# A decoder layer's start: products of x that the norm has not scaled yet, for the first two of eight groups

## The chip, the cores and the metric

The kernel runs on one core of one Trainium2 chip. Its time is device microseconds (us) of one execution. The kernel before the change was run three times: 2462.48, 2463.01 and 2464.7 us, a median of 2463.01. A further execution was taken with the hardware profiler; every row below is from that one.

The engines are named as the profile names them: PE is TensorE (matrix products; PEld its weight loads), DVE is VectorE, ACT is ScalarE, POOL is GpSimd, SP is SyncE, whose queue issues the DMAs.

## What is computed

One layer of a decoder on 1024 prompt tokens and 8 x 8 sample tokens, 1088 in all, with a model width of 2048. The input is normalised and modulated by a scale and a shift that depend on the batch element, then multiplied by one wide input projection; attention, a gated MLP and an mLSTM follow, and an output projection. Only the beginning matters here:

```python
def _rmsnorm(x, g):
    xf = x.astype(jnp.float32)
    y = xf * lax.rsqrt(jnp.mean(xf * xf, axis=-1, keepdims=True) + EPS)
    return (y * g.astype(jnp.float32)).astype(x.dtype)

def _layer(x, c, norm_g, ada_w, ada_b, w_in, ...):
    mod = jax.nn.silu(c.astype(f32)) @ ada_w.astype(f32) + ada_b.astype(f32)
    shift, scale, gate = jnp.split(mod, 3, axis=-1)
    h = (_rmsnorm(x, norm_g).astype(f32) * (1.0 + scale[:, None]) + shift[:, None]).astype(dt)
    proj = h @ w_in
    ...
```

So h = x * r * s + b, with r one factor per token (the norm's), s and b one number per model row and batch element (nine of them: the prompt, and eight sample sequences). The product with the weights is a sum over the 2048 model rows. Because r does not depend on the row, it can be taken out of the sum, and so can the share of b: sum(w * (x*r*s + b)) = r * sum(w * x*s) + sum(w * b).

## The kernel before

**Layout.** x lies transposed: 16 tiles `xs[k]` of 128 model rows by 1088 tokens, 544 KB each. Tokens are worked in three chunks (`CH`: 384, 384 and 320 wide; the last holds the 64 sample tokens). PE multiplies in fp32r, a rounded format; for fp32 accuracy every factor is split into a high and a low part (`wh`, `wl` of the weights, `hH`, `hL` of h), and `products` takes three products: high by high, low by high, high by low. The split of a weight tile is an ACT cast (`wh`, L98) and a POOL subtraction (`wl`, L99) of 128x512.

**The first stage.** The first four column tiles of the projection (`NST` = 4, kept in SBUF sums `accs`) are computed while scale and shift are still being made, in eight groups: group g covers the rows of tiles 2g and 2g+1. One group is 12 units (4 column tiles by 3 chunks) of six matmuls, and after each unit DVE adds the result to its sum (L584). Group 0 is taken in two halves, one row tile at a time (L553).

**Scale and shift.** `ada_group(g)` is a generator that the loops advance step by step. It multiplies the 8 tiles of `adaw` for the group (512 KB each) by the silu of c on PE (L342, "sets" of two tiles; the two halves of group 0 are L353), copies the result (ACT L366), turns it (PE L374), reduces it (DVE L376), makes scale and shift (`modulation`, DVE L409 to L411), applies them to the two x tiles (DVE L420 to L424, then ACT cast to `hH`, L425) and makes `hL` (DVE L431). The table `AT[g]` says behind which unit of group g which later group's generator takes a step.

**The norm's factor.** At the program's start all 16 x tiles are loaded, squared (ACT L389 and DVE L387 by turns) and summed over rows by PE (`token_sums`, L272); `token_rsqrt` makes the factor and spreads it over the partitions (`rbc`). `scaled(k)` multiplies an x tile by it: two on DVE, the other 14 on POOL (L398). Only then come the modulation and the first product.

**Order.** Every engine runs its instructions in the order in which the program wrote them. SP issues all DMAs in such an order too; an issue whose tile is still in use waits, and all behind it wait with it. The `ad` tiles have 4 buffers, the raw weights 4, the split weights 4, the PSUM tiles of products (`mm`) 4.

## Time and profile before

| | us |
|---|---|
| median of 3 runs | 2463.01 |
| profiled execution, its own time | 2462.13 |
| its span, first to last instruction | 2460.1 |
| first product of the first stage begins | 47.22 |
| group 2 (the third) begins its products | 100.99 |
| group 3 (the fourth) begins its products | 119.45 |
| bytes moved by DMA | 332.95 MB |
| granted TensorE clock, mean | 0.997 |

A row of the timeline reads: start, duration, engine, line, operation, output <- inputs, shapes, count; in brackets the idle time before it and what ended it. A row of the windows reads: the stretch, its length, then for each engine busy us and in brackets the instructions, the granted PE clock, the busy share of the DMA engines and the rate in GB/s. A row of the groups reads: line, engine, operation, tiles, shapes, count | busy us, mean ns of one | idle before, and for whom. Durations of instructions that follow each other on one engine can overlap a little, so a row of several is shorter than count times mean.

### The profile page before, as it was taken

The page shows a single profiled execution, that of the slowest core. Times are in us where ns is not written, and L with a number is a line of the kernel's source. Part 1 is how long each engine was busy: PE and PEld are TensorE (multiplying, and loading weights), DVE is VectorE, ACT ScalarE, POOL GpSimd, SP SyncE. Part 2 cuts the span into 40 slices and gives each one's busy share as a digit, 9 for nine tenths or more (in the row PEclk, how much of TensorE's full clock was granted, in tenths as well). Part 3 has the DMA queues.
Part 4 walks back from the last instruction along what each step waited for, and adds up shares of the span by engine and source line. Part 5 has one row for each costly group of instructions (what it writes and reads, how often), then busy time and mean ns, then how long its engine had stood idle before and what let it go on. Part 6 is the DMA issues. An engine that isn't in the chain of part 4 may idle for free.

```text
span 2460.1 us, 39820 instructions
## 1 busy us (share of the span) xinstructions
PE 2419.0 (98%) x15879; PEld 2237.5 (91%) x15879; DVE 923.8 (38%) x2489; ACT 746.1 (30%) x1638; POOL 644.3 (26%) x502
## 2 busy tenths in 40 slices
PE   5899999999999999999999999999999999999999
PEld 2677899999999999999999999888989999999898
DVE  5662300323232231323352001333311688887322
ACT  3222221323323232323321111222212566666210
POOL 2431222232322232222221322121211333332321
PEclk8999999999999999999999999999999999999999
DMA  8774621111121112112411524657565855554454
GB/s 289 255 258 158 220 65 44 57 62 57 54 65 58 53 49 73 38 52 71 127 56 59 172 76 171 223 178 265 188 240 187 255 157 165 152 151 139 164 171 141
DMA packets 157081, 332.95 MB, mean 135 GB/s; under 512 B 21770, under 2 KB 76834, under 8 KB 149216
## 3 DMA queue, kind: packets, MB, share of 16 engines
q1 hardware_dynamic: 156896, 330.41, 41.1%
q8 instruction: 125, 2.05, 0.3%
q14 instruction: 60, 0.49, 0.1%
HBM read 284.26 MB, written 54.55 MB: 138 GB/s over the span
## 4 chain that ended last, share of the span: by engine, by line
PE 95%; DMA 2%; DVE 2%; issue 0%; SPq 0%; ACT 0%; POOL 0%; DVEq 0%; POOLq 0%; ACTq 0%
PE mm L252 27%; PE mm L254 26%; PE mm L253 26%; PE pt L1493 2%; PE ad L342 2%; PE os L1300 1%; PE o L1504 1%; PE sq L1250 1%; PE o L1502 1%; DMA ad<-in_adaw 1%; PE s L1452 1%; PE s L1451 1%; DMA x<-in_xT 1%; PE b L942 0%; PE b L974 0%; PE b L982 0%
## 5 line engine op out<-in xcount | busy, mean ns | idle before, releaser
L252 PE MATMUL mm<-hH,wh 128*128 128x384 f32 (+1 forms) x3168 | 1058.5, 334 | 9.3 <-ACT hH L425 8.1
L253 PE MATMUL mm<-hL,wh 128*128 128x384 f32 (+1 forms) x3168 | 1034.8, 327 | 2.6 <-DVE hL L431 2.6
L254 PE MATMUL mm<-hH,wl 128*128 128x384 f32 (+1 forms) x3168 | 1036.0, 327 | 0.0
L99 POOL TENSOR_TENSOR wl<-wraw,wh 128x512 fp32r<-128x512 f32 x344 | 445.7, 1304 | 1545.8 <-ACT wh L98 1433.4
L252 PEld LDWEIGHTS mm<-hH,wh 128*128 128x128 f32 x3168 | 595.9, 188 | 51.3 <-issue 32.1
L253 PEld LDWEIGHTS mm<-hL,wh 128*128 128x128 f32 x3168 | 596.3, 188 | 4.4 <-DVE hL L431 3.6
L254 PEld LDWEIGHTS mm<-hH,wl 128*128 128x128 f32 x3168 | 595.4, 188 | 0.0
L98 ACT CAST wh<-wraw 128x512 fp32r<-128x512 f32 x344 | 200.8, 596 | 409.6 <-PE mm L253 270.9
L252 PE MATMUL mm<-yH,wh 128*128 128x512 f32 (+2 forms) x768 | 261.7, 341 | 0.0
L254 PE MATMUL mm<-yH,wl 128*128 128x512 f32 (+2 forms) x768 | 251.7, 328 | 0.4 <-POOL wl L99 0.4
L253 PE MATMUL mm<-yL,wh 128*128 128x512 f32 (+2 forms) x768 | 251.7, 328 | 0.0
L254 PEld LDWEIGHTS mm<-yH,wl 128*128 128x128 f32 x768 | 144.8, 189 | 11.7 <-POOL wl L99 0.9
L252 PEld LDWEIGHTS mm<-yH,wh 128*128 128x128 f32 x768 | 145.1, 189 | 9.6
L253 PEld LDWEIGHTS mm<-yL,wh 128*128 128x128 f32 x768 | 145.3, 189 | 9.3
L898 DVE SCALAR_TENSOR_TENSOR u<-R,cw,u 128x384 f32<-128x384 f32 (+1 forms) x108 | 62.0, 574 | 213.3 <-ACT u L896 210.8
L1588 DVE SCALAR_TENSOR_TENSOR xo<-mm,gate,xo 128x512 f32<-128x512 f32 (+2 forms) x96 | 54.5, 569 | 117.4 <-PE mm L254 101.8
L1494 ACT CAST pH<-pt 128x512 fp32r<-128x512 f32 (+1 forms) x120 | 65.3, 544 | 63.3 <-PE pt L1493 62.5
L1495 DVE TENSOR_TENSOR pL<-pt,pH 128x512 fp32r<-128x512 f32 (+1 forms) x120 | 74.8, 623 | 11.6 <-ACT pH L1494 11.2
L1463 ACT ACTIVATE P<-P,mx 128x128 f32<-128x128 f32 (+3 forms) x96 | 74.4, 777 | 1.0 <-DVE mx L1460 1.0
L1493 PE MATMUL pt<-cst,P 128*128 128x128 f32 x432 | 66.6, 272 | 0.0
L1454 DVE CUSTOM_DVE_ANT_0 P<-s,btab 128x384 f32<-128x384 f32 (+2 forms) x96 | 54.7, 570 | 30.0 <-PE s L1452 29.1
L1504 PE MATMUL o<-pL,vh 128*64 128x256 f32 x240 | 61.8, 281 | 1.9 <-DVE pL L1495 1.9
(324 smaller groups left out, 2378.8 us busy)
## 6 DMA issues: line engine op xcount, KB each, us to landing
wraw<-in_win SPq DMA_DIRECT2D x264, 256.0 KB
ad<-in_adaw SPq DMA_DIRECT2D x96, 512.0 KB
kv<-in_ck SPq DMA_DIRECT2D x30, 1024.0 KB
kv<-in_cv SPq DMA_DIRECT2D x30, 1024.0 KB
wraw<-in_wout SPq DMA_DIRECT2D x48, 256.0 KB
x<-in_xT SPq DMA_DIRECT2D x16, 544.0 KB
yraw<-yD SPq DMA_DIRECT2D x16, 544.0 KB
xo<-in_xT SPq DMA_DIRECT2D x16, 544.0 KB
```

Of the source, the lines that this page charges most:

```text
L98: self.nc.scalar.copy(wh[:, :n], raw[:, :n])
L99: self.nc.gpsimd.tensor_tensor(wl[:, :n], raw[:, :n], wh[:, :n].bitcast(FT), op=OP.subtract)
L252: T.matmul(ps[:, :n], wh[:, a], rh[:, t0:t0 + n], start=first and i == 0, stop=False)
L253: T.matmul(ps[:, :n], wh[:, a], rl[:, t0:t0 + n], start=False, stop=False)
L254: T.matmul(ps[:, :n], wl[:, a], rh[:, t0:t0 + n], start=False, stop=last and i == len(rows) - 1)
L898: V.scalar_tensor_tensor(u[:, :npr], R[:, j:j + npr], cw[:, m, j:j + 1], u[:, :npr], op0=OP.mult, op1=OP.add)
L1454: V.tensor_tensor_reduce(s[:, k0:k0 + w], ps[:, :w], e["bt"][:, x:x + w], 1.0, mx[:, np_ - 1:np_] if np_ else -3.0e38, op0=OP.add, op1=OP.max,
L1463: S.activation(s[:, :nk], s[:, :nk], AF.Exp, bias=mx[:, 2:3], accum_out=mx[:, 3:4])
L1493: T.transpose(pt[:, o:o + 128], P[r][:, k:k + 128], ident)
L1494: S.copy(pH[:, f:], pt[:, f:])
L1495: at(0, 3, lambda: V.tensor_tensor(pL[:, f:], pt[:, f:], pH[:, f:].bitcast(FT), op=OP.subtract))
L1504: T.matmul(po[0][0:64, :256], e["vh"][:, kb, 0, :], pL[:, c], start=False, stop=(kb == 2 * m + 1), skip_group_check=True)
```

## The change

Groups 0 and 1 (`NRAW` = 2) multiply x by the scale alone: `raw_high` and `raw_low` make `rH` and `rL` from x * s. Their products go into the sums unscaled. When the norm's factor is there, DVE multiplies each of the 12 pieces of the sums by it (new line in group 2's loop) and adds the shift's share, `ssum`, which `shift_sums` makes with 16 small matmuls per group. The rows of tiles 0 to 3 are needed as true h later, so `scaled`, `high` and `low` make `hH` and `hL` for them during groups 3 to 7.

Squares and their sums move behind the units of group 1 (table `STAT`). In group 2, `high` with `fused` applies scale and factor in one DVE instruction per chunk. `scaled` runs on POOL for all tiles but 4 and 5, in three pieces by chunk. x tiles are loaded in four portions: tile 0 first, tile 1 behind the first four ada tiles, tiles 2 and 3 behind the first half of group 1's ada tiles, and tiles 4 to 15 ahead of most of group 2's. Up to group 4, half of the ada tiles lie in the general slots, so that eight can be on the way instead of four. Groups 0 to 2 take their units by chunk (all four column tiles of a chunk, then the next); before, only group 0 did.

```diff
+    xload(0, 1)
+    W.dma_to(0)
     ada_dma(4)
     W.dma_to(1)
-    for k in range(KT):
...
+    xload(1, 2)
+    ada_dma(8)
...
+    def raw_high(k, c):
...
+        V.tensor_scalar(x[:, a], x[:, a], md[k][:, 1, 0:1], None, op0=OP.mult)
+        if c == 2:
+            per_batch(x, k, 1, OP.mult)
+        S.copy(rH[k][:, t0:t0 + n], x[:, t0:t0 + n])
+
+    def raw_low(k, c):
...
+        V.tensor_tensor(rL[k][:, a], xs[k][:, a], rH[k][:, a].bitcast(FT), op=OP.subtract)
...
+    def scaled(k):
+        for t0, n in CH:
+            a = slice(t0, t0 + n)
+            G.tensor_tensor(xs[k][:, a], xs[k][:, a], rbc[:, a], op=OP.mult)
...
+    def high(k, t0=0, t1=TOK, fused=False):
...
+        if fused:
+            V.scalar_tensor_tensor(x[:, a], x[:, a], md[k][:, 1, 0:1], rbc[:, a], op0=OP.mult, op1=OP.mult)
+        S.activation(hH[k][:, a], x[:, a], AF.Identity, bias=shift(k)[:, 0:1])
...
+    def low(k, t0=0, t1=TOK):
...
+        V.scalar_tensor_tensor(hL[k][:, a], xs[k][:, a], shift(k)[:, 0:1], hH[k][:, a].bitcast(FT), op0=OP.add,
+                               op1=OP.subtract)
...
+    AT[2] = {1: (0, 1), 3: (1,), 4: (0,), 5: (1,), 7: (1,), 8: (1,), 9: (1,), 10: (1,), 11: (1, 2)}
+    AT[3] = {0: (1,), 2: (1,), 4: (1,), 6: (1,), 7: (1,), 8: (1,), 9: (1, 2), 11: (2,)}
...
+    STAT = {(1, 2 * i): (2 * i + 4, 2 * i + 5) for i in range(6)}
+    SCALED = {(2, 0): 6, (2, 2): 7, (2, 6): 8, (2, 9): 9, (3, 1): 10, (3, 4): 11, (3, 7): 0, (3, 10): 1,
+              (4, 1): 12, (4, 4): 13, (4, 7): 2, (4, 10): 3, (5, 1): 14, (5, 4): 15}
...
+            if g == NRAW:
+                V.tensor_tensor(acc, acc, rbc[:, t0:t0 + n], op=OP.mult)
             ps = mm.tile([128, 512], FT, tag="mm", name="mm")
+            products(ps, n, wh[:, a], wl[:, a], hh, t0, True, True)
+            if g != NRAW:
+                V.tensor_tensor(acc, acc, ps[:, :n], op=OP.add)
+            else:
+                m = min(n, NPR - t0)
+                V.scalar_tensor_tensor(acc[:, :m], ps[:, :m], ssum[:, j, 0:1], acc[:, :m], op0=OP.add, op1=OP.add)
...
+            for k, sq in waiting:
+                sums(k, sq)
+            waiting = [(k, square(k)) for k in STAT.get((g, u), ())]
...
+        if g == 1:
+            for k, sq in waiting:
+                sums(k, sq)
+            waiting = []
+            next(root)
+            shift_sums(1, w)
+            next(groups[2])
...
+            G.tensor_copy(shifts[:, 2 * NRAW, 0:1], hL[5][:, 0:1].bitcast(FT))
```

Three places show what moves.

SP's queue at the very start, before the change (`cst` are constants, `csp` the raw c, `x` the x tiles, `ad` the ada tiles, `wraw` raw weights):

```order
L204 DMA cst<-in_cst 128x693
L304 DMA csp<-in_cT 128x16x9
L312 DMA x<-in_xT 128x1088 x16
L326 DMA ad<-in_adaw 128x4x256 x4
L87 DMA wraw<-in_win 128x2x256 x2
L326 DMA ad<-in_adaw 128x4x256 x4
```

The same place in the changed program (`craw` is the raw c, now one contiguous row per partition):

```order
L211 DMA cst<-in_cst 128x693
L311 DMA craw<-in_cT 128x144
L324 DMA x<-in_xT 128x1088
L87 DMA wraw<-in_win 128x2x256
L339 DMA ad<-in_adaw 128x4x256 x4
L87 DMA wraw<-in_win 128x2x256
L324 DMA x<-in_xT 128x1088
L339 DMA ad<-in_adaw 128x4x256 x4
L342 DMA ad<-in_adaw 128x1024 x4
L324 DMA x<-in_xT 128x1088 x2
```

Fifteen of the 16 x tiles have moved behind the first four ada tiles; twelve of them come ten issues after the last row shown.

DVE in the middle of group 2, before (`acc` are the sums, `mm` the products in PSUM; the step of the next group's modulation stands between the adds):

```order
L584 TENSOR_TENSOR acc_232<-acc_232,mm 128x384 x2
L376 TENSOR_REDUCE ads<-at 128x36
L409 TENSOR_TENSOR md<-ads,cst 128x2x9
L410 TENSOR_TENSOR md<-ads,cst 128x2x9
L411 SCALAR_TENSOR_TENSOR md<-md,cst 128x2x9
L420 TENSOR_SCALAR x<-x,md 128x1024
```

DVE in the first half of group 2, now (`rbc` is the norm's factor, `ssum` the shift's share):

```order
L513 SCALAR_TENSOR_TENSOR hL<-x,md,hH 128x384 x2
L702 TENSOR_TENSOR acc_131<-acc_131,rbc 128x384
L709 SCALAR_TENSOR_TENSOR acc_131<-mm,ssum,acc_131 128x384
L702 TENSOR_TENSOR acc_132<-acc_132,rbc 128x384
L709 SCALAR_TENSOR_TENSOR acc_132<-mm,ssum,acc_132 128x384
L499 SCALAR_TENSOR_TENSOR x<-x,md,rbc 128x384 x2
```

One DVE instruction per unit has become two, and the chunks of the group's own h are made between them.

POOL from the first weights on, before (`wl` the low weights, `hL` low parts that POOL made for some chunks):

```order
L99 TENSOR_TENSOR wl<-wraw,wh 128x512 x2
L398 TENSOR_TENSOR x<-x,rbc 128x1088 x4
L431 TENSOR_TENSOR hL<-x,hH 128x384 x2
L431 TENSOR_TENSOR hL<-x,hH 128x320
L99 TENSOR_TENSOR wl<-wraw,wh 128x512 x2
```

And now (the copy into `shifts` only makes POOL wait for the first chunk of group 2's `hL`):

```order
L108 TENSOR_TENSOR wl<-wraw,wh 128x512 x6
L751 COPY shifts<-hL 128x1
L424 TENSOR_TENSOR x<-x,rbc 128x384 x2
L424 TENSOR_TENSOR x<-x,rbc 128x320
L424 TENSOR_TENSOR x<-x,rbc 128x384 x2
```

POOL's scaling of x no longer stands ahead of the first products; it starts inside group 2, in three pieces per tile.

## The prediction

> **What bounds the kernel now.** The page first: busy shares and slices.

> ```profile
> span 2460.1 us, 39820 instructions
> PE 2419.0 (98%) x15879; PEld 2237.5 (91%) x15879; DVE 923.8 (38%) x2489; ACT 746.1 (30%) x1638; POOL 644.3 (26%) x502
> ...
> PE   5899999999999999999999999999999999999999
> ```

> PE is the bound, busy 2419.0 of 2460.1 us. Each digit covers 61.5 us, and only the first two fall below 9: most of the 41 idle us lie early. The windows over the first stage, cut where groups begin, show where.

> ```profile
> core 0: us, PE busy (x) PEld busy (x) DVE busy (x) ACT busy (x) POOL busy (x), PEclk, DMA share, GB/s
> 28.00:47.20 19.20, 9.39 (x83) 4.01 (x83) 12.54 (x19) 4.20 (x9) 9.80 (x5) 0.86 0.95 315
> 47.20:62.50 15.30, 13.76 (x70) 7.85 (x71) 9.44 (x16) 6.76 (x17) 7.42 (x5) 0.73 0.53 161
> 62.50:76.40 13.90, 10.36 (x50) 8.00 (x49) 8.04 (x18) 4.19 (x10) 3.78 (x4) 0.88 0.73 260
> 76.40:101.00 24.60, 21.33 (x127) 13.55 (x126) 14.75 (x31) 5.34 (x9) 13.19 (x10) 1.00 0.59 198
> 101.00:119.40 18.40, 17.75 (x110) 13.05 (x109) 12.93 (x25) 3.90 (x6) 9.15 (x5) 1.00 0.82 296
> 119.40:136.00 16.60, 16.60 (x110) 13.28 (x109) 12.06 (x25) 3.90 (x6) 8.60 (x5) 1.00 0.79 287
> 136.00:152.90 16.90, 16.90 (x110) 13.19 (x109) 11.96 (x25) 3.89 (x6) 8.48 (x5) 1.00 0.78 280
> ```

> From 119.4 on a group takes 16.6 to 16.9 us and PE never rests. Ahead of that, group 0's halves took 15.3 and 13.9 us at granted clocks of 0.73 and 0.88, group 1 24.6, group 2 18.4. What can be won lies ahead of 119.4; from there a lead or a lag goes one to one into the end. So I ask: when does group 3's first unit finish, and what do the groups behind it lose?

> ```profile
> 119.45 0.34 PE L252 MATMUL mm<-hH,wh 128*128 128x384 f32 x1
> ...
> 120.34 0.33 PE L254 MATMUL mm<-hH,wl 128*128 128x384 f32 x1
> ```

> Group 3's first unit is these two and four between, 0.175 apart: before, it was done at 120.6.

> **The change up to group 2.** The old start, in four rows:

> ```profile
> 7.79 1.11 ACT L389 ACTIVATE sq<-x 128x1088 f32<-128x1088 f32 x1 [1.12 <-DMA x<-in_xT]
> ...
> 27.94 0.84 PE L272 MATMUL st<-sq,cst 128*32 128x384 f32 x6 [0.33 <-ACT sq L389]
> ...
> 28.17 1.29 DVE L387 TENSOR_TENSOR sq<-x 128x1088 f32<-128x1088 f32 x1 [1.45 <-DMA x<-in_xT]
> ...
> 47.22 0.69 PE L252 MATMUL mm<-hH,wh 128*128 128x384 f32 x1 [5.45 <-ACT hH L425]
> ```

> Sixteen x tiles of 544 KB landed 1.36 us apart ((28.17 - 7.79)/15), 410 GB/s. Now only x tile 0, 256 KB of weights and four ada tiles (1.3 to 1.4 us each) come ahead of the first scale, so it has its data at 13. Then the chain to a product:

> ```profile
> 39.67 0.64 PE L353 MATMUL ad<-ad,csp 128*32 128x256 f32 x8 [0.63 <-DMA ad<-in_adaw]
> ...
> L366 ACT COPY at<-ad 128x256 f32<-128x256 f32 x16 | 5.3, 376 | 52.3 <-PE ad L342 51.8 <-PE ad L353 0.4
> ...
> 40.24 0.44 PE L374 MATMUL at<-cst,at 128*128 128x128 f32 x2
> ...
> 40.72 0.23 DVE L376 TENSOR_REDUCE ads<-at 128x18 f32<-128x72 f32 x1 [0.31 <-PE at L374]
> ...
> 46.66 0.51 ACT L425 CAST hH<-x 128x384 fp32r<-128x384 f32 x1 [8.01 <-DVE x L420]
> ```

> Set 0.64, copy 0.38, turn 0.44, reduce 0.23, three small DVE instructions about 0.6, scale 0.4, cast 0.51, hand-offs about 0.4: 3.6 us. First product at 16.6, not 47.22.

> Then by steps, as estimates from these rows. First half: 36 products at 0.175 (twice that while the clock is low, 0.73 in the old window) and four sets: 10 us, 26.6. Chain 3.2, second half 9.5, since its adds stand on DVE behind 5 us of `raw_high` and `raw_low`: 39.3. Shift sums 1.6 (16 tiny products, 0.1 each), two sums of squares 1.4, two sets 1.9, chain 3.4: 47.6. Group 1: a pair of units 2.1, two sums of squares 0.65 each; but DVE squares (1.29) behind the add of the pair's first unit, so PE waits some 0.85: 4.25 a pair, six pairs, less 2 for the narrow chunk: 23.5, to 71.1. Last, the root:

> ```profile
> 32.41 0.17 DVE L221 TENSOR_SCALAR rs<-ss 128x9 int32<-128x9 int32 x1
> ...
> 34.25 0.17 DVE L225 SCALAR_TENSOR_TENSOR rs<-rs,rs 128x9 f32<-128x9 f32 x1
> ...
> 34.48 1.86 PE L295 MATMUL rb<-cst,rs 128*128 128x128 f32 x9 [1.75 <-DVE rs L225]
> ```

> Ten steps from 32.41 to 34.42 are 2.0, the spread 1.86; before them copies, shift sums, a set and transposes (3.5), behind them a set, copies, turn and modulation (2.3 with what PE hides): DVE's first fused instruction at 80.8, the first product at 82, **19 ahead** of group 2's old 100.99 (119.45 less the 18.4 of its window). The four chains are known to a second each: 14 to 22.

> The loads hide under this. Ahead of group 2's last ada tile stand 24 MB: at 410 GB/s it lands at about 62, at the 315 of the window with the small pieces at 79, and its set is due at 79. SP's new waits for PE (old ada buffers) stand behind tiles still in flight.

> **Group 2, on DVE.** PE needs some 17 us for it. DVE does not keep up:

> ```profile
> L584 DVE TENSOR_TENSOR acc<-acc,mm 128x384 f32<-128x384 f32 x56 | 30.2, 549 | 23.8 <-PE mm L254 23.6
> ...
> L898 DVE SCALAR_TENSOR_TENSOR u<-R,cw,u 128x384 f32<-128x384 f32 x72 | 44.6, 619 | 203.7 <-ACT u L896 202.0
> ...
> 98.30 1.28 DVE L431 TENSOR_TENSOR hL<-x,hH 128x1088 fp32r<-128x1088 f32 x1
> ...
> 128.30 0.81 DVE L420 TENSOR_SCALAR x<-x,md 128x1024 f32<-128x1024 f32 x1
> ```

> The old add costs 0.549. Now each unit is a rescale at 0.549 and, waiting for it, an add with a scalar like L898's 0.619 (ends overlap by 0.05): 1.13, eight times; the four narrow units, with four instructions, 1.4: 14.6 in all. The group's own h: first chunk 2.4, the other two 5.9. The next group's modulation: 0.9, twice 0.81 + 0.3, twice 1.2, 5.5. Sum **28.4 us** with no wait, in DVE's order, and group 3's first unit needs the last `hL` of it. The old group 2 had 12.93 of DVE.

> To that comes POOL, which scales four tiles and splits two or three weight tiles meanwhile. What that does, the old trace shows:

> ```profile
> 75.12 4.05 POOL L431 TENSOR_TENSOR hL<-x,hH 128x384 fp32r<-128x384 f32 x4
> ...
> 75.30 0.94 DVE L553 TENSOR_TENSOR acc<-acc,mm 128x384 f32<-128x384 f32 x2
> ...
> 76.16 1.20 DVE L420 TENSOR_SCALAR x<-x,md 128x256 f32<-128x256 f32 x1
> ...
> 77.28 1.02 DVE L423 TENSOR_TENSOR x<-x,md 128x64 f32<-128x64 f32 x1
> ...
> 79.50 0.21 DVE L423 TENSOR_TENSOR x<-x,md 128x64 f32<-128x64 f32 x1
> ```

> Four POOL pieces of 384 ran from 75.12 to 79.17. DVE's adds out of PSUM did not notice. L423 took 1.02 under them and 0.21 after: an instruction that lives in SBUF alone waits for one POOL piece. Group 2 has 15 POOL pieces of about 1 us. If DVE's next SBUF instruction always meets one, as here, about 0.65 of each is lost, +9.8; if pieces fall under PSUM adds and gaps, nothing. I take +6, nearer the row: 34.4. Group 3's first unit is done at 80.8 + 34.4 + 0.4 = 115.6, **5 ahead** of 120.6 (1 to 11).

> [...]

> **Behind group 2.** In group 3, POOL has two weight tiles and four x tiles (0, 1, 10, 11), 14 us instead of 8.6. The second pair falls on the chain that makes group 4's h, eleven SBUF instructions, five to seven of which meet a piece; 1.2 us of it are slack: 0 to -4.5, I take -3.5. In groups 4 and 5 the pieces end ahead of the chain, by its unit: 0. The extra `high` and `low` of tiles 0 to 3 lie on ACT and in DVE's free 4.6 us a group. Eight ada tiles on the way instead of four: a group's content is 11.9 of products, 3.85 of sets and 0.44 of turn, 16.2, against 16.6 and 16.9: +1.2 over three groups (0 to 2). PE's clock, idle in group 2:

> ```profile
> 66.27 0.33 PE L253 MATMUL mm<-hL,wh 128*128 128x384 f32 x1
> ...
> 69.10 1.11 PE L374 MATMUL at<-cst,at 128*128 128x128 f32 x4 [2.33 <-ACT at L366]
> ...
> 70.33 0.52 PE L253 MATMUL mm<-hL,wh 128*128 128x384 f32 x1
> ...
> 73.03 0.33 PE L254 MATMUL mm<-hH,wl 128*128 128x384 f32 x1
> ```

> After an idle 2.33 the products took 0.52, and 0.33 again by 73.03. Group 3 may start so: 0 to -1.7, I take -0.7.

> [...]

> **Sum**: 5 - 3.5 + 1.2 - 0.7 = 2 us less than the profiled execution's 2462.13 (its span and 2.03 around it): 2460.1. That execution lay 0.9 below the median of the runs, so **2461**.

> **Rivals.** (a) *The lock costs little*: pieces by chunk fit under PSUM adds, group 2 takes 29 to 30 on DVE, group 3 loses 1. Lead 10 - 1 + 1 - 0.5 = 9.5: about 2453 (2449 to 2457). For it: only 12 of the SBUF instructions of group 2 stand outside the chains, and POOL starts late. Against it: the 1.02 row. (b) *Slower, by the lock*: every SBUF instruction of group 2 meets a piece (38.2), group 3 loses 4.5, the clock 1.7, and the start comes 2 late: lead 1 - 4.5 - 1.7 - 2 + 0.5 = -6.7: about 2469. It ends above the old time once DVE's group 2 lasts over 36 us. (c) *The early start is not there*, for want of data: x behind ada tiles makes group 1 wait. By the 410 GB/s tile 15 lands at 55, needed at 68; only under 315 would it decide: 2466 or so.

> **How the numbers follow.** Forecast 0.41, (a) 0.34, (b) 0.21, (c) 0.04. A measurement can tell 0.2%, 4.9 us: faster is (a), 0.34; slower (b) and (c), 0.25; same 0.41. The range takes in most of (a) and (b): 2450 to 2471; the forecast alone 2458 to 2467.

> **What would show it.** First product near 17 and not 47; group 2's first at 79 to 87; DVE busy without a gap from there for 30 to 38 us while PE falls to about half; rescales of acc longer than 0.55 where POOL runs; group 3's first unit at 110 to 119. I am wrong if group 1 waits for x, or if group 2 goes at PE's pace.

## The result

The changed kernel takes 2484.53 us, median of 4 runs (2482.16 to 2486.69), beside 2463.24 for the kernel before (4 runs): a ratio of 1.0081, 95% interval 1.0069 to 1.0093. It is 21 us slower; the forecast was 2461, with a range up to 2471. The profiled execution ran 2482.16 us, its span 2480.4.

The page of the changed kernel, busy shares and slices of 62 us:

```profile
span 2480.4 us, 39969 instructions
PE 2428.9 (98%) x15911; PEld 2244.8 (91%) x15911; DVE 941.6 (38%) x2550; ACT 752.0 (30%) x1654; POOL 641.7 (26%) x522
PE   7799999999999999999999999999999999999999
```

The first slice rose from 5 to 7, the second fell from 8 to 7. The windows of the changed kernel, cut where group 0's halves, group 1, the chain to the norm's factor and groups 2, 3, 4 and 5 begin:

```profile
core 0: us, PE busy (x) PEld busy (x) DVE busy (x) ACT busy (x) POOL busy (x), PEclk, DMA share, GB/s
18.80:32.40 13.60, 11.78 (x77) 8.14 (x77) 4.78 (x15) 7.15 (x17) 0.00 (x0) 1.00 1.05 394
32.40:50.70 18.30, 15.86 (x100) 11.25 (x100) 11.34 (x29) 4.28 (x10) 2.54 (x2) 0.91 0.84 314
50.70:75.00 24.30, 22.96 (x144) 13.52 (x144) 17.88 (x34) 9.47 (x15) 2.58 (x2) 1.00 0.77 303
75.00:86.70 11.70, 8.43 (x68) 4.42 (x65) 4.65 (x20) 2.92 (x8) 0.00 (x0) 1.00 0.65 222
86.70:114.20 27.50, 21.32 (x116) 14.46 (x116) 24.93 (x49) 5.97 (x13) 16.72 (x15) 0.94 0.78 286
114.20:143.60 29.40, 22.19 (x116) 14.71 (x116) 19.31 (x34) 4.65 (x8) 15.93 (x14) 0.77 0.24 78
143.60:165.10 21.50, 19.33 (x112) 14.31 (x109) 15.21 (x26) 5.76 (x9) 11.94 (x10) 0.92 0.71 238
165.10:183.00 17.90, 17.80 (x110) 12.88 (x108) 13.65 (x26) 5.16 (x8) 14.23 (x14) 1.00 0.79 260
```

The first product is there at 18.8 instead of 47.2, as meant. Then the lead is eaten: group 2 takes 27.5 us (18.4 before), group 3 29.4 (16.6), group 4 21.5 (16.9). In group 3 PE is busy for 22.2 of 29.4 us, and at a granted clock of 0.77. (The 1.00 of the first row is no evidence: the trace's record of the clock begins at 22.3, and PE's products from 18.8 to 22 start 0.32 us apart, as they do at half rate further on.) The starts of products in PE's timeline give the account. The last two rows count only products of 128 by 128 weights:

| first product of | before | changed | lead (-) or lag |
|---|---|---|---|
| group 0 | 47.2 | 18.8 | -28.4 |
| group 1 | 76.4 | 50.7 | -25.7 |
| group 2 | 101.0 | 86.8 | -14.2 |
| group 3 | 119.5 | 114.3 | -5.2 |
| (end of group 3's first unit) | 120.67 | 123.63 | +3.0 |
| group 4 | 136.0 | 143.7 | +7.7 |
| group 5 | 152.9 | 165.1 | +12.2 |
| group 7 | 185.5 | 199.0 | +13.5 |
| 72 products after group 7's first | 214.4 | 229.2 | +14.8 |
| 360 more products on | 299.6 | 319.3 | +19.7 |

Group 3's beginning, in PE's timeline of the changed kernel:

```profile
114.28 0.55 PE L259 MATMUL mm<-hH,wh 128*128 128x384 f32 x1 [4.37 <-ACT hH L525]
118.17 0.69 PE L260 MATMUL mm<-hL,wh 128*128 128x384 f32 x1 [3.35 <-DVE hL L529]
...
122.62 0.69 PE L260 MATMUL mm<-hL,wh 128*128 128x384 f32 x1 [3.12 <-DVE hL L529]
...
123.56 1.94 PE L355 MATMUL ad<-ad,csp 128*32 128x512 f32 x8
125.43 0.69 PE L259 MATMUL mm<-hH,wh 128*128 128x384 f32 x1
125.91 0.53 PE L260 MATMUL mm<-hL,wh 128*128 128x384 f32 x1
126.23 0.53 PE L261 MATMUL mm<-hH,wl 128*128 128x384 f32 x1
```

The rows show three waits for h, and behind them work at half rate: eight products of an ada set took 1.94 us (1.07 in the next set), and products start 0.32 us apart where 0.175 is usual. What DVE did from the first fused instruction to the last `hL` of group 2, by groups:

```profile
L702 DVE TENSOR_TENSOR acc<-acc,rbc 128x384 f32<-128x384 f32 x8 | 6.2, 777 | 0.0
L709 DVE SCALAR_TENSOR_TENSOR acc<-mm,ssum,acc 128x384 f32<-128x384 f32 x8 | 4.9, 617 | 1.9 <-PE mm L261 1.3
L499 DVE SCALAR_TENSOR_TENSOR x<-x,md,rbc 128x384 f32<-128x384 f32 x4 | 3.7, 977 | 0.1
L529 DVE TENSOR_TENSOR hL<-x,hH 128x1088 fp32r<-128x1088 f32 x2 | 3.4, 1684 | 0.0
```

It was busy for 34.1 of 37.1 us (85.44 to 122.57), and PE's last wait above ends with its last `hL`: DVE sets group 2's end. So three things can cost the 21 us: DVE's own new work, POOL's lock on it (the name here for what DVE's timeline shows: L702 took 1.64 us at 95.80, beside POOL's split of a weight tile, and 0.55 at 98.08, where POOL rested), and the clock behind PE's waits.

### The profile page after: what moved, and what is told of

Read it like the earlier page. It is cut to its first block, busy times and chain, and to the rows that moved or that the text cites. A ratio compares the mean times of both kernels' runs of the same rounds, so it can differ in the third digit from the quotient of the medians.

```text
span 2480.4 us, 39969 instructions
## 1 busy us (share of the span) xinstructions
PE 2428.9 (98%) x15911; PEld 2244.8 (91%) x15911; DVE 941.6 (38%) x2550; ACT 752.0 (30%) x1654; POOL 641.7 (26%) x522
## 4 chain that ended last, share of the span: by engine, by line
PE 93%; DVE 4%; DMA 1%; issue 1%; ACT 1%; SPq 0%; POOL 0%; DVEq 0%; ACTq 0%; POOLq 0%
PE mm L259 26%; PE mm L260 25%; PE mm L261 25%; PE pt L1649 2%; DMA ad<-in_adaw 1%; PE ad L355 1%; PE os L1456 1%; PE o L1660 1%; PE o L1658 1%; PE sq L1406 1%; PE s L1608 1%; PE s L1607 1%; DVE hL L529 1%; PE b L1098 0%; PE b L1130 0%
## 5 line engine op out<-in xcount | busy, mean ns | idle before, releaser
L259 PE MATMUL mm<-hH,wh 128*128 128x384 f32 (+1 forms) x3120 | 1044.1, 335 | 9.3 <-ACT hH L525 4.4
L260 PE MATMUL mm<-hL,wh 128*128 128x384 f32 (+1 forms) x3120 | 1021.0, 327 | 11.2 <-DVE hL L529 10.1
L261 PE MATMUL mm<-hH,wl 128*128 128x384 f32 (+1 forms) x3120 | 1021.4, 327 | 0.0
L259 PEld LDWEIGHTS mm<-hH,wh 128*128 128x128 f32 x3120 | 587.6, 188 | 54.8 <-issue 30.1
L260 PEld LDWEIGHTS mm<-hL,wh 128*128 128x128 f32 x3120 | 588.1, 189 | 14.5 <-DVE hL L529 12.2
L261 PEld LDWEIGHTS mm<-hH,wl 128*128 128x128 f32 x3120 | 587.4, 188 | 0.0
```

Source lines behind the costliest of these rows:

```text
L259: T.matmul(ps[:, :n], wh[:, a], rh[:, t0:t0 + n], start=first and i == 0, stop=False)
L260: T.matmul(ps[:, :n], wh[:, a], rl[:, t0:t0 + n], start=False, stop=False)
L261: T.matmul(ps[:, :n], wl[:, a], rh[:, t0:t0 + n], start=False, stop=last and i == len(rows) - 1)
```

## The experiments

Times are medians; the ratio is to the kernel before on the chip of that run (2464.7 to 2465.3 there). Gains of e1 to e4 are counted from the changed kernel's 2484.53, those of the later runs from e8's 2484.78. Four kernels do less work than the layer needs: e1 leaves out the scaling of x, e2 the multiplication of the sums, e6 and e14 both.

| run | edit | us | ratio, 95% interval |
|---|---|---|---|
| e1 | no scaling on POOL | 2474.34 | 1.0035, 1.0022 to 1.0048 |
| e2 | no multiplication of acc | 2478.00 | 1.0045, 1.0029 to 1.0062 |
| e3 | ada sets by two | 2487.09 | 1.0091, 1.0075 to 1.0106 |
| e4 | tiles 0 to 3 scaled later | 2483.30 | 1.0069, 1.0054 to 1.0084 |
| e8 | changed kernel again | 2484.78 | 1.0073, 1.0056 to 1.0089 |
| e5 | gate's requests as before | 2481.94 | 1.0065, 1.0050 to 1.0080 |
| e6 | e1 + e2 + e5 | 2467.07 | 1.0006, 0.9996 to 1.0015 |
| e7 | PE kept busy in its waits | 2475.42 | 1.0039, 1.0024 to 1.0054 |
| e11 | multiplications of acc moved | 2480.68 | 1.0063, 1.0050 to 1.0075 |
| e12 | squares added by pairs | 2487.24 | 1.0088, 1.0075 to 1.0101 |
| e9 | e4 + e5 + e7 + e11 + e12 | 2474.52 | 1.0034, 1.0022 to 1.0046 |
| e10 | kernel before, PE kept busy | 2465.75 | 1.0004, 0.9996 to 1.0013 |
| e14 | e6 and PE kept busy | 2454.86 | 0.9962, 0.9949 to 0.9976 |
| e13 | group 2 into sums of its own | 2463.00 | 0.9994, 0.9985 to 1.0002 |
| e15 | e13, scaling off the chains | 2461.55 | 0.9985, 0.9976 to 0.9994 |

### The lock and DVE's own work: e1, e2

```diff
-            if (g, u) in SCALED:
-                scaled(SCALED[g, u])
```

> GpSimd multiplies no tile of x by the norm's factor (the 42 pieces of L424 are left out; all else stays). Theory lock: those pieces hold DVE up, by some 7.6 us in group 2 (sum of what DVE's SBUF instructions took there above their undisturbed times), by 3 in the chains that make the h of groups 4 and 5, and each PE wait of over 3 us is followed by 2 us of products at half clock. Then the time falls by 11 to 17 us, to 2468 to 2474, DVE's group 2 (first fused instruction to last hL) goes from 37.1 to about 29, and group 4's waits for hL are gone. Rival own work: DVE's own instructions of group 2 are the cost and the lock hides beside PE: at most 3 us fall, 2482 or more.

It fell by 10.2 us, a little under the range. DVE's group 2 now lasts 32.2 us (88.72 to 120.89), against 37.1 in the changed kernel. The same groups as above, in e1:

```profile
L702 DVE TENSOR_TENSOR acc<-acc,rbc 128x384 f32<-128x384 f32 x8 | 5.1, 642 | 0.0
L709 DVE SCALAR_TENSOR_TENSOR acc<-mm,ssum,acc 128x384 f32<-128x384 f32 x8 | 4.9, 618 | 2.7 <-PE mm L261 2.1
...
L529 DVE TENSOR_TENSOR hL<-x,hH 128x1088 fp32r<-128x1088 f32 x2 | 2.6, 1285 | 0.0
...
L499 DVE SCALAR_TENSOR_TENSOR x<-x,md,rbc 128x384 f32<-128x384 f32 x4 | 2.3, 614 | 0.1
```

The lock (a DVE instruction on tiles in SBUF takes longer while a POOL piece runs) shows in the means: L499 977 against 614 ns, L529 1684 against 1285, L702 777 against 642; L709, which reads PSUM, 617 against 618. The lock of the scaling costs group 2 5.0 us. What keeps DVE above the 29 expected are 2.1 us of waits for PE, and POOL's splits of weights, which still lock: the four narrow multiplications of acc (128x320) took 754 ns on average here (one of them 1.57 us, at 117.15), and 480 in the changed kernel where no piece ran (112.96 and 115.45); beside a split alone (117.39 to 119.24) one took 1.56 us there. Behind group 2 there is more: from the end of group 3's first unit to group 7's first product e1's profiled execution takes 69.8 us, e8's (the changed kernel again) 74.0.

```diff
-            if g == NRAW:
-                V.tensor_tensor(acc, acc, rbc[:, t0:t0 + n], op=OP.mult)
```

> The twelve multiplications of acc by the norm's factor in group 2 (L702) are left out. Theory own work: DVE sets the pace of group 2, so the 6.3 us that they take undisturbed, and up to 3 us of lock that they met, come off the end: 2475 to 2479. Rival: the tiles that GpSimd scales for group 3 (6 and 7) or the weight tiles that it splits arrive last, and DVE only fills the time: 2482 or more.

It fell by 6.5 us (2478.0), as the theory had it: DVE's own work is on the path too.

### Two ideas that gave nothing: e3, e4

```diff
-            ada_set(ps, s_)
+            if g < 3 or g >= 8:
+                ada_set(ps, s_)
+            elif s_ % 2:
+                ada_set(ps, s_ - 1)
+                ada_set(ps, s_)
```

> In groups 3 to 7 the sets of ada are issued two at a time again, at the second of the two places (eight products of a set cost 1.0 us and about 0.2 of switching at each break). Theory sets: each break costs 0.2 to 0.25 us, two fewer in each of groups 2 to 6 as they are run: 2 to 2.5 us fall, 2482. Rival: the breaks cost nothing that is not idle anyway (DVE or GpSimd set the pace of groups 3 and 4): within 1 us of 2484.5.

2487.09: the expected 2 us did not come, and it is above what the rival allowed too. A set that is issued later also reaches its chain later; that this is the reason is not shown.

```diff
-    SCALED = {(2, 0): 6, (2, 2): 7, (2, 6): 8, (2, 9): 9, (3, 1): 10, (3, 4): 11, (3, 7): 0, (3, 10): 1,
-              (4, 1): 12, (4, 4): 13, (4, 7): 2, (4, 10): 3, (5, 1): 14, (5, 4): 15}
...
+              (4, 1): 12, (4, 4): 13, (5, 1): 14, (5, 4): 15,
+              (5, 7): 0, (5, 10): 1, (6, 1): 2, (6, 4): 3}
```

> The scaling of tiles 0 to 3 on GpSimd moves from groups 3 and 4 to groups 5 and 6, their high and low parts with it. Theory lock, by place: the second pair of tiles in group 3 lies on the chain that makes group 4's h (2.3 us of PE waiting and 1.8 us of products at half clock behind it, a wait of 0.7 for an add), so 4 to 6 us fall: 2479 to 2480. Rival: the first pair alone (tiles 10 and 11) holds the chain up as much, or the pieces cost the same in groups 5 and 6: within 1.5 us of 2484.5.

2483.30 is within the rival's 1.5 us. The lock moved with the pieces: beside e8, groups 3 to 5 take 64.6 us instead of 67.4, but groups 6 and 7, which now hold the scaling, 32.8 instead of 30.2.

### The gate's requests: e5

```diff
             if s_ < 3 and (g < 8 or s_ % 2):
+                if g >= 8:
+                    ada_dma(used[0] + 4)
                 yield
                 if g >= 8:
-                    ada_dma(used[0] + 4)
                     yield
+        if g >= 8:
+            ada_dma(used[0] + 4)
```

> The changed kernel once more, as it is, beside which the next three are read on this chip. Its ratio to the kernel before should be 1.007 to 1.009 again. It also tells how much of its start differs between executions: in the profile of the changed kernel group 1 (second) took 36.0 us with no product at half clock in its first unit, in the four runs so far 37.9 to 39.4 with some.

This run, e8, came out at 2484.78, a ratio of 1.0073; from group 1's first product to group 2's it took 39.3 us, as the four runs ahead of it and not as the first profile (36.0).

> The order of the requests for ada tiles of groups 8 to 11 (the gate's) is put back as it was before the change: all four next tiles are asked for as soon as a pair of sets is issued, not two of them one unit later. Theory late requests: the 4.9 us that the changed kernel lost on the old one between the second column after the groups and the sixth (229.2 to 319.3 against 214.4 to 299.6) come from these requests, and 3 to 5 us go. Rival: they come from the traffic that then runs (other loads and stores of the gate stage, met 15 to 20 us later), and it stays within 1.5 us of the changed kernel.

e5 is 2.8 us below e8, just under the 3 to 5 expected, and the intervals of the two ratios overlap; the trace is clearer. The same 360 products, windows of the kernel before, the changed kernel and e5:

```profile
214.40:299.60 85.20, 84.49 (x539) 67.30 (x538) 23.80 (x50) 26.97 (x48) 17.48 (x15) 1.00 0.65 227
```

```profile
229.20:319.30 90.10, 86.36 (x538) 67.55 (x538) 23.88 (x50) 27.17 (x48) 16.62 (x15) 1.00 0.63 214
```

```profile
231.60:318.30 86.70, 84.57 (x538) 67.44 (x538) 23.77 (x50) 26.94 (x48) 17.50 (x15) 1.00 0.64 223
```

PE's work is 84 to 86 us in all three; of the 4.9 us lost, 3.4 are back. The changed generator asked for two of the four next ada tiles one unit later, and PE waited 3.1 us for one of them; in e5 the longest such wait is still 1.9. The trace favours late requests; the times alone would not settle it.

### All three, and the clock: e6, e7, e14, e10

> No scaling on GpSimd (L424 left out), no multiplication of acc by the norm's factor (L702 left out), and the gate's requests as before the change. If the three terms stand apart, their gains add up: 11 + 9 + 4 = 24 us less than the changed kernel, 2460, under the kernel before. If the first two fill the same time on DVE in group 2 (the theory that DVE alone sets its pace would still have both, one after the other), 15 to 18 less, 2467 to 2470. DVE's group 2 should last 32.1 - 6.3 = 26 us or less.

17.7 us less than e8, where the theory had 15 to 18 for gains that partly fill the same time (the parts add up to 10.2 + 6.5 + 2.8 = 19.5), and yet only level with the kernel before. DVE's group 2 lasts 26.8 us. The windows of groups 2, 3 and 4:

```profile
91.10:111.50 20.40, 20.15 (x116) 14.01 (x116) 14.77 (x40) 6.01 (x12) 2.81 (x3) 0.92 0.85 314
111.50:137.20 25.70, 21.76 (x121) 14.75 (x117) 15.54 (x33) 5.51 (x8) 3.90 (x3) 0.87 0.37 118
137.20:155.40 18.20, 18.20 (x113) 12.98 (x110) 12.73 (x24) 4.85 (x7) 3.35 (x2) 1.00 0.83 301
```

DVE is no longer full (14.8 of 20.4 us), but group 2 starts at 91.1, as in e8, and group 3 takes 25.7 us at a clock of 0.87. The clock itself was tested by products that nobody reads, in PE's queue where it waits:

```diff
+    def warm(n, wt, xt):
+        ps = bank("wm")
+        for _ in range(n):
+            T.matmul(ps[:, :384], wt[:, 0:128], xt[:, 0:384], start=True, stop=True)
```

> Products that nobody reads are put into PE's queue where it waits at the start: 8 ahead of the second half of group 0, 8 ahead of group 1, 10 ahead of group 2, and 22, 16 and 14 ahead of group 3 and inside its first unit, each 128x384. Theory clock: a PE that has waited 2 us or more runs its next products at about half the rate for some 3.3 us (0.32 instead of 0.175 us apart), a loss of 1.5 to 3 us at each of five places; kept busy it loses nothing, and the time falls by 5 to 8 us against the changed kernel. Rival: the low clock lies in time that PE would wait for DVE anyway (its next wait only grows), or the fillers overrun: within 2 us, or slower.

9.4 us less than e8, a little over the range. Windows of groups 2 and 3 in e7:

```profile
87.70:114.20 26.50, 24.26 (x139) 16.73 (x139) 24.91 (x49) 5.93 (x12) 17.30 (x15) 1.00 0.78 285
114.20:141.10 26.90, 24.33 (x146) 18.02 (x146) 19.31 (x34) 4.69 (x7) 16.02 (x14) 1.00 0.27 86
```

The clock is 1.00 in both, group 2 begins 3.5 us earlier than e8's (91.2), and DVE's work (24.91, 19.31) is what it was: the rate of PE is what changed. Then both together:

> No scaling on GpSimd (L424 left out), no multiplication of acc (L702 left out), the gate's requests as before, and fillers where PE waits (10, 9, 8 and 10 ahead of the first four waits, 12 and 8 inside group 3's first unit). Theory clock: what e6 left is PE's half rate behind its waits (five places of some 1.5 us in its products, as much again in its sets and first rows), so 6 to 9 us less than e6's 2467: 2458 to 2461, under the kernel before. Rival: something else holds groups 2 and 3: 2465 or more.

2454.86: 12.2 us less than e6, more than the 6 to 9 expected. Group 3's first unit ends at 110.3, where the kernel before had 120.7. This accounts for the size of the loss: the gains of e1, e2, e5 and e7 alone add up to 28.9 us (10.2 + 6.5 + 2.8 + 9.4), and together, in e14, they are 29.9. What is then left of the early start is 10 us; but e14 leaves out work that the layer needs, so it bounds the gain and is no kernel to use. On the kernel before, fillers changed nothing:

> The kernel before the change with 26 fillers ahead of its first product (PE waited 5.45 us there) and 12 ahead of the second unit of group 1 (2.62 us). Theory clock: its first half group ran at a granted clock of 0.73 (13.8 us of products), of which the first 3 to 4 us at half rate, and about 1 behind the other wait: 1.5 to 4 us less than the kernel before. Rival: group 0's pace was DVE's and the waits only move: within 1 us.

2465.75 against 2464.79, within 1 us, as the rival had it. But this run does not test what full clock would be worth there, for the half rate stayed:

```profile
46.29:49.70 3.41, 1.25 (x6) 0.67 (x4) 2.83 (x2) 0.51 (x1) 3.41 (x2) 1.00 0.00 0
49.71:56.53 6.82, 5.38 (x22) 2.04 (x23) 3.51 (x7) 2.08 (x5) 0.97 (x1) 0.50 0.27 79
```

The 26 fillers ended at 47.1, the first product began at 48.9 (47.2 without fillers), and PE waited 1.8 us more for `hL` behind it. Group 0 took 28.8 us instead of 29.2, with another wait of 2.9 for the turn of an ada set. Whether PE's rate matters in the kernel before stays open.

### Where DVE's work stands: e11, e12, e9, e13, e15

```diff
+            rescale(V, 0)
             next(groups[2])
             next(groups[2])
...
+            rescale(G, 1)
+            rescale(G, 2)
```

> The multiplications of acc by the norm's factor leave DVE's loop of group 2: the four of the first chunk go into the 3.6 us in which DVE waits for the turned ada set ahead of group 2, the eight others to GpSimd, ahead of its scaling of tiles 6 and 7. Theory DVE-bound: group 2 loses DVE's 6.3 us and gets part of them back as lock (eight more pieces of about 1 us on GpSimd): 3 to 7 us less than the changed kernel. Rival: each piece on GpSimd costs DVE what the multiplication cost it, or tiles 6 and 7 come too late for group 3: within 2 us of the changed kernel, or slower.

4.1 us less than e8, within the range; leaving them out altogether gave 6.5 (e2).

```diff
+                if u < 10:
+                    G.tensor_tensor(sq[0], sq[0], sq[1], op=OP.add)
+                    waiting.append((12 * g + u + 3, sq[0]))
```

> In group 1 the squares of two tiles are added on GpSimd (idle there) before their sums are taken, for five of the six pairs: PE issues 15 products of 128x384 or 128x320 with 32 columns fewer, 0.42 us and a start for each tile. Theory: group 1 is PE's own work, and the sums of squares, which the old kernel took while it waited for x, now stand in it: 2 to 4 us less than the changed kernel. Rival: GpSimd's additions (3 us each) hold up DVE's squares and rL, and group 1 gets no shorter: within 1 us, or slower.

There was no gain. The waits of PE in e12's group 1 say why:

```profile
PE st L279 <- POOL sq L719: 6.7, 3, 3.3
```

An addition took POOL 2.5 us and PE came to its sums before it was done, three times: the saved products were paid back in waiting.

> All that the runs so far point to, in one kernel that computes everything: fillers where PE waits (10 ahead of the first product, 9, 8 and 10 ahead of the next three waits, 10, 6 and 8 at group 3), the gate's requests as before the change, tiles 0 to 3 scaled in groups 5 and 6, the multiplications of acc moved, squares added by pairs. If the gains stood apart: 9 + 3 + 1.5 + 3 to 7 + 2 to 4, 19 to 24 us less than the changed kernel, 2461 to 2466, no more than the kernel before. If fillers and moved multiplications win the same time: 2467 to 2471.

2474.52 is no better than e7 alone (2475.42) and above both expected ranges. It carries e12's waits (7.2 us in its group 1), and the half rate behind them is back; that its fillers and moved multiplications also win the same time is likely, but not shown.

Then DVE was taken out of group 2's loop:

```diff
+            if g == NRAW:
+                if c == 0:
+                    acc2.append(slot("acc2"))
+                S.copy(acc2[j][:, t0:t0 + n], ps[:, :n])
...
+    def merge(j, c):
...
+        V.scalar_tensor_tensor(a[:, :m], a[:, :m], ssum[:, j, 0:1], b[:, :m], op0=OP.add, op1=OP.add)
```

> Everything is computed. Group 2's products go from PSUM to sums of their own by ScalarE, so that DVE has nothing to do with acc in its loop but four multiplications; the multiplications and additions of the two kinds of sums follow one by one through groups 3 to 5, four multiplications of the first chunk in DVE's wait ahead of group 2. Fillers at the first four waits, the gate's requests as before, tiles 0 to 3 scaled in groups 5 and 6. Theory place: group 2 is then PE's (17 to 20 us instead of 27.5), group 3 starts at about 108 with waits of 1 to 3 us, the twelve merges (about 1.2 us each) use up DVE's slack of groups 3 to 5 and cost 2 to 5: 2454 to 2462, faster than the kernel before. Rival lock: GpSimd's scaling, which stays, holds DVE's chains up wherever they are, and groups 3 to 5 lose what group 2 wins: 2466 to 2475.

2463.0: 21 us faster than the changed kernel, level with the one before, and 1 us above the theory's range. Not all of it is due to the second sums: e13 also has the fillers, e5's order of requests and e4's places for tiles 0 to 3, which alone gave 9.4 (e7, with other numbers of fillers), 2.8 and 1.2. Its group 2 took 22.2 us, not 17 to 20. DVE's chain for group 3 in e13:

```profile
100.80 1.05 DVE L436 TENSOR_TENSOR md<-ads,cst 128x18 f32<-128x18 f32 x1
101.88 0.80 DVE L437 SCALAR_TENSOR_TENSOR md<-md,cst 128x18 f32<-128x18 f32 x1
102.78 1.39 DVE L522 TENSOR_SCALAR x<-x,md 128x1024 f32<-128x1024 f32 x1
```

These are instructions of 0.17, 0.18 and 0.81 us, each held by a piece of POOL's (99.82 to 105.83), and PE waited 3.3 us behind them. So the pieces were moved to each group's first units:

```diff
+    SCALED = {(2, 0): 6, (2, 1): 7, (2, 2): 8, (3, 0): 9, (3, 2): 10, (4, 0): 11, (4, 2): 12, (5, 0): 13, (5, 2): 14,
+              (5, 4): 15, (6, 0): 0, (6, 2): 1, (6, 10): 2, (6, 11): 3}
```

> As the kernel with second sums (e13), with the scaling of tiles moved to the first units of each group, ahead of the chain that makes the next group's h (tiles 6, 7, 8 in group 2, two in groups 3 and 4, three in group 5, 0 and 1 at the start of group 6, 2 and 3 at its end), the high and low parts of tiles 0 to 3 in group 7, and the last three sets of group 3's ada one unit earlier. Theory lock by place: the waits of 3.3, 1.4 and 3 us and the half rate behind the first go, 4 to 8 us less than e13's 2463: 2455 to 2459, ratio to the kernel before 0.996 to 0.998. Rival: the lock costs the same wherever the pieces lie, since DVE is never free in groups 2 to 6: within 2 us of e13.

2461.55. Its windows of groups 2, 3 and 4:

```profile
85.90:106.00 20.10, 19.04 (x116) 12.84 (x116) 18.48 (x33) 9.48 (x22) 14.35 (x12) 1.00 0.92 319
106.00:126.00 20.00, 18.89 (x117) 12.94 (x117) 14.49 (x28) 6.35 (x11) 8.27 (x9) 1.00 0.48 150
126.00:144.80 18.80, 17.44 (x112) 12.76 (x109) 18.17 (x32) 3.82 (x6) 12.25 (x9) 1.00 0.83 289
```

Groups 2 and 3 take 40.1 us where e13 took 44.2, as the theory had it. But group 5, with three tiles to scale, takes 19.8 (18.0 in e13), and groups 6 and 7 with the narrow products behind them 50.2 (49.6; 44.2 in the kernel before), so that most of it is lost again: 1.5 us better than e13, the rival's size, and no more than the intervals of the two. It is the one kernel here that computes everything and beats both, by 0.15% of the kernel before (interval 0.06% to 0.24%).

## Why the prediction was wrong

In the profiled executions the forecast had group 3's first unit 5 us ahead of the kernel before and 3 us of that lost behind it, so 2 ahead at the end. It was 3.0 behind there and 20 at the end: 8 us were missed up to that unit (4.8 in the start, 2.7 in DVE's group 2, 0.5 in the step to PE) and about 14 behind it.

**The start, 14 to 22 ahead, taken 19.** It was 14.2 in the profiled execution, 4.8 short: the first product came at 18.8 instead of 16.6 (the last ada tile of the first scale landed at 14.0, not 13, and the first modulation, 0.84 us instead of 0.17, met a POOL subtraction), and the second half, group 1 and the root were late by another 2.6 in small parts. That execution was lucky: in seven others with the same start, group 2 began at 89.7 to 91.2; their traces show PE at half rate in group 1's first unit as well.

**Loads.** Right: PE waited for no x tile, and the rival of a start starved of data did not occur.

**Group 2 on DVE.** Right in kind, nearly in size: 28.4 without waits and 6 of lock, 34.4 in all; it was 37.1. e1 gives the lock of the 12 scaling pieces as 5.0, where 0.65 us for each, the forecast's full price, would be 7.8: DVE's additions out of PSUM ran beside the pieces (617 ns with them, 618 without), and not every instruction in SBUF met one (L522 took its 0.81 us). The rest is waits for PE and the lock of weight splits.

**Behind group 2: the step that failed.** The forecast let group 3 and the later stages lose 3.5 to the lock and 0.7 to the clock, and gain 1.2 by the deeper prefetch: 3 us. It was 16.7 (from 3.0 behind at group 3's first unit to 19.7). Its terms:

- *The clock* was the term mis-sized most, counted over the whole kernel. The forecast had it at half rate in group 0's first half and at 0.7 us for group 3's products. In the profiled execution it struck at five places, from 18.8, 32.5, 87.2, 114.5 and 148.6 us on, and slowed sets as well as products. Keeping PE busy was worth 9.4 us with all else as it was (e7) and 12.2 with DVE relieved (e6 to e14). By the profiled executions of e7 and e8, 4.9 us of it are won up to the end of group 3's first unit, and 2.4 from there to group 4.
- *The prefetch's gain* of 1.2 turned into a loss of as much. In e14, with PE at full clock and hardly waiting, groups 4 to 6 take 50.7 us, before 49.5; in group 4 PE is then busy with ada sets for 5.48 us (36 products), before for 4.39 (32); the sets now come one at a time, not in twos.
- *The gate's requests* were not priced at all. They cost about 3 us by the medians of e5 and e8, at the far end of a change that seemed to concern the start.
- *The lock in groups 3 to 5*, taken as 3.5, is real (1.39 us for an instruction of 0.81 in e13) and nearly of that size: without the scaling these groups and group 6 are 4.2 us shorter (e1 beside e8, with what half rate follows).

These four come to about 11 of the 16.7 us (2.4 + 1.2 + 3 + 4.2). The rest stays open: in groups 3 and 4 the lock, the waits and the half rate stand side by side, and no run takes them apart.

**The rivals.** The point given for "slower, by the lock" (DVE's group 2 over 36 us) was passed, with 37.1, and the sign was that rival's; its 2469 was still 15 too low, as it too took 1.7 us for the clock and nothing for the gate. Its mechanism was not borne out either: the lock of group 2 was not at its most (above).

## What to carry to other kernels

When work is brought forward, what was hidden in the old wait (here the norm's sums and its factor) goes into time that the bound engine owns, and the engine that helps it has to be added up instruction by instruction in the group that takes the new work: an average of 38% busy said nothing of the 37 us in which DVE set the pace. A wait of the bound PE cost more here than itself: behind one of 1.81 us PE's products ran at half rate for 3.3 us more (at 32.4 in the changed kernel's profile). Where the end of such a wait is not in one's hands, products that nobody reads are worth trying (they gave 9.4 us here, e7). On the kernel before they stopped 1.9 us short of the end of the wait, the half rate stayed, and nothing was gained (e10). A generator that is rewritten for one stage is to be compared step by step in every stage that uses it: the order in which it asks for data is part of what it does.

## What the runs showed of the hardware

```profile
32.40 0.58 PE L259 MATMUL mm<-rH,wh 128*128 128x384 f32 x1 [1.81 <-ACT rH L458]
32.99 0.69 PE L260 MATMUL mm<-rL,wh 128*128 128x384 f32 x1
33.48 0.52 PE L261 MATMUL mm<-rH,wl 128*128 128x384 f32 x1
...
36.01 0.34 PE L260 MATMUL mm<-rL,wh 128*128 128x384 f32 x1
```

It is not the same in each execution: behind the wait of 1.97 us that ends at 50.74 that profile shows no slow product, behind the same wait e1's shows nine. Where the two differ can be read from the granted clock. In the profiles of the two kernels it changes only in steps of 3.41 us: in that of the kernel before, from 14.36 to 72.39, it holds one rate for 20.48, 3.41, 6.83, 10.24, 13.65 and 3.41 us, all multiples of 3.41. Here are some of these steps, two pairs of the changed kernel and one of e1:

```profile
29.13:32.54 3.41, 1.60 (x17) 0.59 (x9) 1.23 (x6) 1.24 (x3) 0.00 (x0) 1.00 1.05 390
32.55:35.95 3.40, 3.39 (x10) 2.99 (x11) 2.30 (x9) 1.62 (x4) 0.00 (x0) 0.50 0.78 312
...
46.20:49.61 3.41, 2.07 (x17) 0.65 (x9) 0.73 (x4) 0.65 (x2) 0.00 (x0) 1.00 1.03 415
49.62:53.02 3.40, 2.12 (x11) 1.87 (x12) 2.29 (x7) 1.94 (x3) 0.00 (x0) 1.00 1.03 408
```

```profile
48.77:52.18 3.41, 0.93 (x7) 0.49 (x5) 1.61 (x7) 1.30 (x4) 0.00 (x0) 1.00 1.02 410
52.19:55.59 3.40, 3.40 (x10) 3.05 (x11) 1.81 (x4) 1.27 (x2) 0.00 (x0) 0.50 1.03 406
```

Behind the step in which PE was busy for 1.60 of 3.41 us, and behind the one with 0.93, comes a step at 0.50; the same wait of 1.97 us, cut by the border of two steps, left 2.07 and 2.12 us of work in them, and no step at half rate followed. In the first 340 us of the 17 profiles the half rate begins 82 times, 71 of them behind a step with PE busy for less than half (in the profiles of the two kernels all seven, with 0.11 to 1.67 us of work), and only 4 such steps have full rate behind them (one with 1.60 us, from 309.02 in the changed kernel); ten of the other eleven beginnings follow a step that holds the shift sums' products of 128x18. So what a wait cost here depended not only on its length but also on where it fell. Keeping PE busy in its waits was worth 9 to 12 us (e7; e6 to e14), 0.4 to 0.5% of the time, about half of what the change lost.

A DVE instruction of 0.17 us on a few numbers (18 per partition) took up to 1.05 us beside a POOL piece (e13), six times its length: on that chain the lock cost 0.88, 0.62 and 0.58 us at three steps in a row, no less at the two of 18 numbers than at the one of 1024.
